# Merging the delta rule's inverted triangles for both directions at once, over four 32x32 array tiles in turn

## The chip, the cores and the metric

The kernel runs on one core of a Trainium2 chip. The metric is the device time of one execution in microseconds (us), from the first instruction to the last. Before the change three timed runs took 2108.64, 2114.71 and 2114.74 us, so the median is 2114.71 us.

The core has these engines: TensorE (PE in the rows; PEld is its loading of weights), VectorE (DVE), ScalarE (ACT), GpSimd (POOL) and SyncE (SP), which here only starts DMAs. Each engine takes its instructions in the order in which they stand in its own stream. TensorE's clock has two levels, 1.2 and 2.4 GHz; the rows give the granted clock as a share of the higher one, so 0.50 is 1.2 GHz.

## The reference, cut to what matters

Two layers of a diffusion backbone: a mixer (softmax attention beside a bidirectional gated delta rule) and a mixture of experts. 256 context tokens and 512 latent tokens make six token tiles of 128; the delta rule has 8 heads of width 64 and works in chunks of 64 tokens, forward and backward. Each chunk, head and direction needs the inverse of a unit lower triangle of 64x64:

```python
def gated_delta_chunked(q, k, v, g, beta, s0):
    ...
    lower = jnp.where(strict, jnp.einsum("bhnid,bhnjd->bhnij", kb, kc) * decay, 0.0)
    eye = jnp.eye(CHUNK, dtype=f32)
    tmat = lax.linalg.triangular_solve(lower + eye, jnp.broadcast_to(eye, lower.shape),
                                       left_side=True, lower=True, unit_diagonal=True)
    u = jnp.einsum("bhnij,bhnje->bhnie", tmat, vc * bc)
    ...
    s_final, o = lax.scan(step, s0, xs)

def hybrid_mixer(h_lat, h_ctx, lp, rope, ctx_out):
    ...
    for d in range(2):
        ...
        o_l, _ = gated_delta_chunked(*(rev(t) for t in (...)), s_c)
```

## The kernel before, in words

**The inverse.** The 64x64 triangle is cut into two 32x32 triangles on the diagonal and one 32x32 block beside them. With the diagonal inverses X0 and X1 and the block U, the missing corner of the inverse is -X1 U X0 (its mirror image in the other direction). `intra_batch` and `delta_intra` make the triangles (with the block kept in a tile `uo`), `delta_subst` inverts all 32x32 triangles of a batch on VectorE by substitution (31 steps of a product `sT` and a subtraction `sY`), and `delta_merge` makes the corner and writes the whole inverse to DRAM (`xad`). The token tiles go through in three batches of two tiles, `PAIRS`; below m0, m1 and m2 are the merges of the three batches, and s0 to s2 their substitutions. A layer has three batches and two directions, so six calls of `delta_merge`.

**One merge before.** The substitution's result goes to DRAM (`dy`, L825) and comes back in another layout as `yl` (L833, two DMAs per direction); VectorE transposes it in 32x32 blocks to `yt` (L834); ScalarE puts the diagonal blocks into the output tile `xm` (L838, two instructions). Then TensorE makes the first product in PSUM (L846, tile `mg`): 16 blocks (two token tiles by eight heads) on one 32x32 tile of the array, then ScalarE copies those 32 partitions, negated, to SBUF (L847), then the same 16 blocks for the other half of the partitions on another array tile and a second copy. The second product (L850) and its copies into `xm` (L851) follow in the same manner. One matmul of fp32 counts as two in the trace's rows, so 16 blocks are x32 there. Last the DMA to `xad` (L853).

**Buffers.** `yl`, `yt`, `xm` and the SBUF tile `mg` have one buffer each (`YL = 1`, `XM = 1`), so a merge waits for the one ahead of it. PSUM has three pools: three banks "a", three banks "c", and one buffer "s" of two banks. The two directions of a batch take a half of "s" each, except for m2 of layer 0, which takes banks of "c" (`MPS`). Attention's scores (`sc`, L603) also take "s", the only buffer of it.

**The order of work.** A string `ORDER` says in which order the pieces are written out (convolutions c, intra i, substitution s, projections n, merges m); a scheduler with a timeline model then sets the order on each engine, so instructions of several pieces interleave. After the merges come 12 delta steps (`delta_step`: pz L916, su L931, ks and pq L897, po L947), woven with attention slots and with the matmuls of the modulation (`aps` L264, from weights `araw`). The steps load the inverse (`lx` L864) and keys and values (`lk` L863) by the SP queue, behind the stores of the merges.

Of the kernel before, what the change touches and what calls it, by code (L numbers as in the profile page):

```python
# [23 lines left out]
P = 128  # L24
# [76 lines left out]
WH = 3  # L101
GV = 2
QS = 1
UO = 10
VR = 1
SB = 2
YB = 2
# [10 lines left out]
EV = (0,)  # L118
EP = (1, 3, 5, 7)
ST = 2  # L120
XM = 1
DDB = 2
FINP = (8, 9, 10, 11)
MPS = ((0, 1), (0, 1, 2))
ORDER = ("c4 c5 c6 c7 S i0 s0 i1 s1 i2 s2 c0 c1 c2 c3 Q n256 n0 x n512 m0 m1 c8 c10 c11 c9 n2304 m2",
         "c4 c5 c6 c7 S c0 i0 s0 i1 s1 c9 i2 s2 c1 c2 c3 Q n256 n0 x n512 m0 m1 c8 c10 n2304 c11 m2")
WP = 3
# [16 lines left out]
class Model:  # L144
# [638 lines left out]
    def delta_intra(self, tt, d, kk, sc, uo, xad, db, pool):  # L783

        nc = self.nc
        gx = pool.tile([P, NH, HD], F32, tag="gx", bufs=1, name="gx")
        nc.gpsimd.tensor_tensor(gx, sc["gr"][:, d, tt, :, None].to_broadcast([P, NH, HD]), self.C["run%d" % d][:, None, :].to_broadcast([P, NH, HD]), op=OP.mult)
        pg = self.psC("gb")
        nc.tensor.matmul(pg, self.C["same"], gx.rearrange("p h i -> p (h i)"), start=True, stop=True)
        dd = pool.tile([P, 512], F32, tag="dd", bufs=DDB, name="dd")  # L790
        d3 = dd.rearrange("p (h i) -> p h i", i=HD)
        nc.vector.tensor_tensor(d3, pg.rearrange("p (h i) -> p h i", i=HD), sc["gcum"][:, d, tt, :, None].to_broadcast([P, NH, HD]), op=OP.subtract)
        nc.vector.tensor_tensor(d3, d3, self.C["mask%d" % d][:, None, :].to_broadcast([P, NH, HD]), op=OP.min)
        nc.scalar.activation(dd, dd, AF.Exp)
        nc.gpsimd.tensor_tensor(d3, d3, sc["bp"][:, d, tt, :, None].to_broadcast([P, NH, HD]), op=OP.mult)
        u = pool.tile([P, 512], F32, tag="u", bufs=2, name="u")
        nc.vector.tensor_tensor(u, kk, dd, op=OP.mult)
        self.q("idd").dma_start(xad[tt, d, :, 1], dd)
        u3 = u.rearrange("p (h i) -> p h i", i=HD)
        qb = 1 - d  # L800
        nc.scalar.activation(uo, u3[:, :, 32 * qb:32 * qb + 32], AF.Copy)
        ud = pool.tile([P, NH, 32], F32, tag="ud", bufs=2, name="ud")
        nc.scalar.activation(ud, u3[:, :, 0:32], AF.Copy, scale=self.C["quad"][:, 0:1])
        nc.vector.scalar_tensor_tensor(ud, u3[:, :, 32:64], self.C["quad"][:, 1:2], ud, op0=OP.mult, op1=OP.add)
        src = ud
        if d == 1:
# [17 lines left out]
            nc.vector.tensor_tensor(Y[:, j + 1:32, 0:w], Y[:, j + 1:32, 0:w], T3, op=OP.subtract)  # L824
        self.q("iy").dma_start(dy.rearrange("h q r c -> (h q) r c"), Y)  # L825

    def delta_merge(self, tts, d, dy, us, xad, ps, pool):

        nc = self.nc
        yt = pool.tile([P, 2, NH, 32], F32, tag="yt", bufs=1, name="yt")  # L830
        yl = pool.tile([P, 2, NH, 32], F32, tag="yl", bufs=YL, name="yl")
        for t in range(2):
            self.q("ild").dma_start(yl[:, t], dy[:, 4 * t:4 * t + 4].rearrange("h q r c -> (q r) h c"))  # L833
        nc.vector.transpose(yt, yl)  # L834
        xb, xt = (yt, yl) if d == 0 else (yl, yt)
        x = pool.tile([P, 2, NH, HD], F32, tag="xm", bufs=XM, name="xm")
        for q in range(2):
            nc.scalar.activation(x[:, :, :, 32 * q:32 * q + 32], xb, AF.Copy, scale=self.C["quad"][:, q:q + 1])  # L838
        qa, qb = (0, 1) if d == 0 else (1, 0)
        cb = slice(32 * qb, 32 * qb + 32)  # L840
        g = pool.tile([P, 512], F32, tag="mg", bufs=1, name="mg")
        place = [(32 * (2 * c2 + qa), 32 * (2 * c2 + qb)) for c2 in range(2)]
        blocks = [(t, h, slice((t * NH + h) * 32, (t * NH + h + 1) * 32)) for t in range(2) for h in range(NH)]
        for ra, rb in place:
            for t, h, c in blocks:
                nc.tensor.matmul(ps[rb:rb + 32, c], us[tts[t], d][ra:ra + 32, h, :], xt[ra:ra + 32, t, h, :], start=True, stop=True, tile_position=(ra, rb))  # L846
            nc.scalar.activation(g[rb:rb + 32], ps[rb:rb + 32], AF.Copy, scale=-1.0)  # L847
        for ra, rb in place:
            for t, h, c in blocks:
                nc.tensor.matmul(ps[ra:ra + 32, c], g[rb:rb + 32, c], xb[rb:rb + 32, t, h, :], start=True, stop=True, tile_position=(rb, ra))  # L850
            nc.scalar.activation(x[ra:ra + 32, :, :, cb], ps[ra:ra + 32].rearrange("p (t h i) -> p t h i", t=2, h=NH), AF.Copy)  # L851
        a, b = tts
        self.q("ix").dma_start(xad[a:b + 1:b - a, d, :, 0].rearrange("t p f -> p t f"), x.rearrange("p t h i -> p t (h i)"))  # L853

    def step_load(self, s, vk, xad, qkd, need, pool):

# [134 lines left out]

    def intra_batch(self, b, us, dT, sc, xad, db, pool):
        kk = [self.delta_kk(tt, 1, dT, pool) for tt in PAIRS[b]]
        for d in range(2):
            for j, tt in enumerate(PAIRS[b]):
                us[tt, d] = pool.tile([P, NH, 32], F32, tag="uo", bufs=UO, name="uo")
                n = 4 * (2 * d + j)
                self.delta_intra(tt, d, kk[j], sc, us[tt, d], xad, db[:, n:n + 4], pool)

    def merge_batch(self, i, b, us, xad, dy, pool):  # L1000
        ps = self.psS("mg") if b in MPS[i] else None
        for d in range(2):
            self.delta_merge(PAIRS[b], d, dy[:, 8 * d:8 * d + 8], us, xad, ps[:, 512 * d:512 * d + 512] if ps is not None else self.psC("mg"), pool)


    def gate(self, mp, ps, n, dst):
# [495 lines left out]
    def layer(self, i, xsrc, rows, done, xstack, mod):  # L1502
# [20 lines left out]
        with self.pool("hp", B) as hp:  # L1523
            with self.pool("pj", B) as wp:
# [47 lines left out]
                with self.pool("pp", B) as pool, self.pool("q1", A) as p1:  # L1572
# [7 lines left out]
                    for op in ORDER[i].split():  # L1580
# [3 lines left out]
                        elif kind == "Q":  # L1584
                            query_norms()
                        elif kind == "c":
                            f = int(arg)
                            if f in (0, 4):
                                ss = self.psS("ss")
                            value_conv(f, pool) if f >= 8 else key_conv(f, ss, pool)  # L1590
                        elif kind == "i":
                            self.intra_batch(int(arg), us, dT, sc, xad, db[int(arg)], p1)
                        elif kind == "s":
                            self.delta_subst(int(arg), db[int(arg)], dy[int(arg)], p1)
                        elif kind == "m":
                            self.merge_batch(i, int(arg), us, xad, dy[int(arg)], p1)
# [172 lines left out]
```

## Time and profile before

| | |
|---|---|
| median of three runs | 2114.71 us |
| profiled execution | 2130.51 us |
| its span | 2128.7 us |
| mean granted clock of TensorE | 0.897 |
| TensorE busy | 1824.3 us (86%) |
| VectorE busy | 1272.6 us (60%) |
| ScalarE busy | 893.5 us (42%) |
| GpSimd busy | 839.5 us (39%) |

Busy shares are averages over stages with different limits. The stage of this change lies, in layer 0, between about 120 and 400 us of the span, and in layer 1 between about 1190 and 1466 us. In a row of the timeline, the first number is the start in us, the second the time in us; a bracket gives the idle time of the engine ahead of it and what ended that.

### The profile page before, as it was taken

Reading aid. Unit: us, or ns where it says so; the run is one execution under the profiler, and the core shown is the slowest. Engines: PE = TensorE matmul, PEld = TensorE weight load, DVE = VectorE, ACT = ScalarE, POOL = GpSimd, SP = SyncE. Lnnn points to the kernel's source line nnn. Section 1 sums busy time; section 2 is a strip of 40 time slices with the busy share of each in tenths; the row PEclk is TensorE's granted clock in tenths of the full one; section 3 lists DMA queues with packets and bytes.
Section 4 is the critical chain, followed back from the end, with each engine's and each line's share of the span. In section 5 each row is a group of like instructions: output and inputs, shape, how many; then the busy total and the mean of one; then the engine's idle time right before and its main releaser. Section 6 shows DMA issues by size and latency. Waiting matters only on the chain. (4 is left out here: it accounts for less than half of the span.)

```text
span 2128.7 us, 34974 instructions
## 1 busy us (share of the span) xinstructions
PE 1824.3 (86%) x13579; PEld 1349.2 (63%) x13579; DVE 1272.6 (60%) x2344; ACT 893.5 (42%) x1531; POOL 839.5 (39%) x915
## 2 busy tenths in 40 slices
PE   6998798888868789999978987767888769999995
PEld 4887687666657655565547876656566555566553
DVE  3469996566672645555546689963676443444443
ACT  3444245655541134444425543334464223444442
POOL 4456653244354323223326376520333632223221
PEclk9999897798988889999998988766998779999997
DMA  8222435787655588889924224356862568888872
GB/s 278 72 71 79 127 117 175 233 230 237 199 135 131 198 329 329 323 320 328 331 65 140 80 71 120 107 170 182 252 186 70 174 265 307 326 315 302 314 263 85
DMA packets 227684, 427.77 MB, mean 201 GB/s; under 512 B 83720, under 2 KB 157180, under 8 KB 202939
## 3 DMA queue, kind: packets, MB, share of 16 engines
q1 hardware_dynamic: 171547, 329.09, 45.9%
q0 software_dynamic: 33536, 72.59, 12.1%
q10 hardware_dynamic: 22432, 23.81, 3.3%
q8 instruction: 109, 1.79, 0.3%
q14 instruction: 60, 0.49, 0.1%
HBM read 386.82 MB, written 84.67 MB: 221 GB/s over the span
## 5 line engine op out<-in xcount | busy, mean ns | idle before, releaser
L1351 PE MATMUL pab<-w,xt 128*128 128x512 f32 x1024 | 465.5, 598 | 0.5 <-ACT xt L1345 0.5
L1351 PEld LDWEIGHTS pab<-w,xt 128*128 128x128 f32 x1024 | 189.7, 192 | 191.3 <-issue 186.5
L1405 POOL DMA_INDIRECT yd<-ey,idx x64 | 116.8, 1824 | 472.3 <-DMA yd<-ey,idx 196.9
L1372 DVE TENSOR_TENSOR gl<-gt,gh 128x256 fp32r<-128x256 f32 x64 | 27.1, 424 | 276.1 <-ACT gh L1371 272.5
L1330 DVE TENSOR_TENSOR w2l<-w,w2h 128x2048 fp32r<-128x2048 f32 x64 | 147.4, 2303 | 44.4 <-ACT w2h L1329 43.0
L1371 ACT ACTIVATE gh<-gt 128x256 fp32r<-128x256 f32 x64 | 24.5, 383 | 348.9 <-PE gt L1367 348.9
L238 PE MATMUL pn<-whi,hh 128*128 128x256 f32 (+1 forms) x432 | 133.9, 313 | 15.3 <-ACT gev L1541 11.4
L488 POOL TENSOR_TENSOR wlo<-wraw,whi 128x1024 fp32r<-128x1024 f32 (+1 forms) x44 | 112.0, 2547 | 82.8 <-ACT whi L487 81.9
L238 PE MATMUL po<-woh,m 128*128 128x512 f32 x320 | 113.0, 431 | 27.8 <-ACT woh L1068 20.6
L238 PE MATMUL pn<-whi,hl 128*128 128x256 f32 (+1 forms) x432 | 133.4, 313 | 0.7 <-DVE hl L349 0.4
L238 PE MATMUL pn<-wlo,hh 128*128 128x256 f32 (+1 forms) x432 | 133.0, 309 | 0.6 <-POOL wlo L488 0.6
L238 PE MATMUL pt<-hh,wlo 128*128 128x512 f32 (+1 forms) x352 | 125.4, 356 | 0.0
L238 PE MATMUL pt<-hh,whi 128*128 128x512 f32 (+1 forms) x352 | 124.3, 353 | 0.0
L238 PE MATMUL pt<-hl,whi 128*128 128x512 f32 (+1 forms) x352 | 123.8, 352 | 0.0
L1329 ACT ACTIVATE w2h<-w 128x2048 fp32r<-128x2048 f32 x64 | 121.7, 1902 | 0.0
L1393 PE MATMUL py<-w2h,gh 128*128 128x512 f32 x256 | 107.7, 421 | 4.4 <-DVE ey L1400 4.4
L1345 ACT ACTIVATE xt<-xt 128x512 f32<-128x512 f32 x128 | 69.7, 595 | 86.8 <-PE xt L1344 86.0
L517 DVE SCALAR_TENSOR_TENSOR dT<-xin,cw,dT 128x772 f32<-128x772 f32 x64 | 79.4, 1243 | 42.2 <-ACT dT L515 40.5
L238 PEld LDWEIGHTS pn<-whi,hh 128*128 128x128 f32 x432 | 90.1, 210 | 20.8 <-ACT gev L1541 12.1
L1393 PE MATMUL py<-w2l,gh 128*128 128x512 f32 x256 | 101.6, 397 | 0.0
L1393 PE MATMUL py<-w2h,gl 128*128 128x512 f32 x256 | 101.2, 395 | 0.0
L1344 PEld LDWEIGHTS xt<-cst,xe 128*128 128x128 f32 x512 | 67.9, 192 | 50.2 <-issue 29.8
(391 smaller groups left out, 4561.8 us busy)
## 6 DMA issues: line engine op xcount, KB each, us to landing
w<-w SPq DMA_DIRECT2D x192, 1024.0 KB, 10.0
araw<-ada_w POOLq DMA_DIRECT2D x40, 1024.0 KB, 9.3
wraw<-w_in SPq DMA_DIRECT2D x40, 512.0 KB, 4.1
lk<-vk SPq DMA_DIRECT2D x48, 256.0 KB, 7.2
lx<-xad SPq DMA_DIRECT2D x40, 256.0 KB, 9.3
araw<-ada_w SPq DMA_DIRECT2D x8, 1024.0 KB, 11.8
wr<-w_out SPq DMA_DIRECT2D x8, 1024.0 KB, 15.4
vk<-vr ACTq DMA_DIRECT2D x16, 384.0 KB, 3.2
```

The source lines that it names most:

```text
L238: self.nc.tensor.matmul(ps, a(k), b(k), start=(first and n == 0), stop=(last and n == 3 * nk - 1))
L488: getattr(nc, eng).tensor_tensor(lo, raw, hi, op=OP.subtract)
L517: nc.vector.scalar_tensor_tensor(dst, xin[:, tap:tap + 772], cw[:, tap, f:f + 1], dst, op0=OP.mult, op1=OP.add)
L1329: self.pin(nc.scalar.activation(hi, src, AF.Copy))
L1330: self.pin(eng.tensor_tensor(lo, src, hi, op=OP.subtract))
L1344: pin(nc.tensor.transpose(ps[:, k * P:(k + 1) * P], xe.rearrange("p (q k) -> p k q", k=8)[:, 4 * q + k, :], self.ident))
L1345: pin(nc.scalar.activation(xt[:, 4 * q:4 * q + 4, :], ps.rearrange("p (k n) -> p k n", k=4), AF.Copy))
L1351: self.pin(self.nc.tensor.matmul(pa.rearrange("p (a f) -> p a f", a=2), xt[:, k, :], w13[:, :, k, :], start=(k == 0), stop=(k == 7)))
L1371: pin(nc.scalar.activation(gh, p3, AF.Copy))
L1372: pin(nc.vector.tensor_tensor(gl, p3, gh, op=OP.subtract))
L1393: pin(self.nc.tensor.matmul(py[:, n * 512:(n + 1) * 512], a[:, j, :], b[:, c], start=(j + m == 0), stop=(j == 1 and m == 2)))
L1405: self.pin(self.nc.gpsimd.indirect_dma_start(out=yd, out_offset=bass.IndirectOffsetOnAxis(ap=idx, axis=0), in_=y, in_offset=None, bounds_c ...
```

## The change

`delta_merge` now takes both directions of a batch in one call. All four loads of `yl` are issued together into a tile of twice the size, one VectorE instruction transposes both, and one loop over the 16 blocks issues four matmuls per block: two directions by two halves, on the array tiles (row, column) (0, 32), (64, 96), (32, 0) and (96, 64). All four write to one PSUM bank, `pa`, on different partitions. One ScalarE instruction copies all 128 partitions. The second product goes in the same manner to the other bank of "s", `pb`, and is no longer copied by ScalarE: VectorE adds it, masked, to `xm`, one instruction per direction over all partitions, each followed by the store to `xad`.

The block U of both directions now shares one tile per token tile: direction d fills the partitions that start at 32d and 64 + 32d, by two ScalarE instructions of 32 partitions in place of one of 128. `UO` is 6 instead of 10. `XM` and `MPS` go: both output tiles `xm` have the one buffer that the tag has, and every merge takes "s".

```diff
-        qb = 1 - d
-        nc.scalar.activation(uo, u3[:, :, 32 * qb:32 * qb + 32], AF.Copy)
+        for r in (32 * d, 64 + 32 * d):
+            nc.scalar.activation(uo[r:r + 32], u3[r:r + 32, :, 32 - 32 * d:64 - 32 * d], AF.Copy)
...
-    def delta_merge(self, tts, d, dy, us, xad, ps, pool):
+    def delta_merge(self, tts, dy, us, xad, pool):
...
+        yt = pool.tile([P, 2, 2, NH, 32], F32, tag="yt", bufs=1, name="yt")
+        yl = pool.tile([P, 2, 2, NH, 32], F32, tag="yl", bufs=YL, name="yl")
+        for d in range(2):
+            for t in range(2):
+                n = 4 * (2 * d + t)
+                self.q("ild").dma_start(yl[:, d, t], dy[:, n:n + 4].rearrange("h q r c -> (q r) h c"))
         nc.vector.transpose(yt, yl)
...
+        xb, xt = (yt[:, 0], yl[:, 1]), (yl[:, 0], yt[:, 1])
+        x = [pool.tile([P, 2, NH, HD], F32, tag="xm", bufs=1, name="xm") for d in range(2)]
...
+        ps = self.psS("mg")
+        pa, pb = ps[:, :512], ps[:, 512:]
+        place = [(d, 32 * (2 * c2 + d), 32 * (2 * c2 + 1 - d)) for d in range(2) for c2 in range(2)]
...
-        for ra, rb in place:
-            for t, h, c in blocks:
-                nc.tensor.matmul(ps[rb:rb + 32, c], us[tts[t], d][ra:ra + 32, h, :], xt[ra:ra + 32, t, h, :], start=True, stop=True, tile_position=(ra, rb))
-            nc.scalar.activation(g[rb:rb + 32], ps[rb:rb + 32], AF.Copy, scale=-1.0)
...
+        for t, h, c in blocks:
+            for d, ra, rb in place:
+                nc.tensor.matmul(pa[rb:rb + 32, c], us[tts[t]][ra:ra + 32, h, :], xt[d][ra:ra + 32, t, h, :], start=True, stop=True, tile_position=(ra, rb))
+        nc.scalar.activation(g, pa, AF.Copy, scale=-1.0)
+        for t, h, c in blocks:
+            for d, ra, rb in place:
+                nc.tensor.matmul(pb[ra:ra + 32, c], g[rb:rb + 32, c], xb[d][rb:rb + 32, t, h, :], start=True, stop=True, tile_position=(rb, ra))
         a, b = tts
+        for d in range(2):
+            y = x[d][:, :, :, 32 - 32 * d:64 - 32 * d]
+            nc.vector.scalar_tensor_tensor(y, pb.rearrange("p (t h i) -> p t h i", t=2, h=NH), self.C["quad"][:, d:d + 1], y, op0=OP.mult, op1=OP.add)
+            self.q("ix").dma_start(xad[a:b + 1:b - a, d, :, 0].rearrange("t p f -> p t f"), x[d].rearrange("p t h i -> p t (h i)"))
```

The scheduler sets a new order from the substitutions on. On TensorE, at the end of m2 in layer 1, this stands before (each row is a run of matmuls; `mg<-yl,uo` and `mg<-yt,uo` are first products of the forward and the backward direction, `mg<-yt,mg` and `mg<-yl,mg` second products):

```order
L846 MATMUL mg<-yl,uo 32x32 x32
L850 MATMUL mg<-yt,mg 32x32 x32
L846 MATMUL mg<-yt,uo 32x32 x32
L850 MATMUL mg<-yl,mg 32x32 x32
L603 MATMUL sc<-ka,qs 128x512
```

and at the same place now (the first product's last rows and the second's first; a row is a direction's two halves):

```order
L848 MATMUL mg<-yl,uo 32x32 x2
L848 MATMUL mg<-yt,uo 32x32 x2
L848 MATMUL mg<-yl,uo 32x32 x2
L848 MATMUL mg<-yt,uo 32x32 x2
L852 MATMUL mg<-yt,mg 32x32 x2
L852 MATMUL mg<-yl,mg 32x32 x2
```

The number of matmuls is the same, 128 a batch; directions and halves now alternate, and two products take the place of four. On the SP queue, which stores and loads around m1 and m2 of layer 1, this stands before:

```order
L825 DMA dy_1_10416<-sY 128x1024
L833 DMA yl<-dy_1_10416 128x8x32 x2
L853 DMA xad_10410<-xm 128x2x512
L833 DMA yl<-dy_1_10416 128x8x32 x2
L853 DMA xad_10410<-xm 128x2x512
L825 DMA dy_1_10417<-sY 128x1024
L1018 DMA gw<-gd_10419 128x512 x2
L833 DMA yl<-dy_1_10417 128x8x32 x2
```

and now:

```order
L823 DMA dy_1_10394<-sY 128x1024
L834 DMA yl<-dy_1_10394 128x8x32
L857 DMA xad_10388<-xm 128x2x512
L834 DMA yl<-dy_1_10394 128x8x32 x3
L1018 DMA gw<-gd_10397 128x512 x2
L857 DMA xad_10388<-xm 128x2x512
L823 DMA dy_1_10395<-sY 128x1024
L834 DMA yl<-dy_1_10395 128x8x32
L857 DMA xad_10388<-xm 128x2x512
L834 DMA yl<-dy_1_10395 128x8x32 x3
```

Three of a batch's four loads stand behind the second direction's store of the batch ahead. In layer 0 the order on TensorE moves attention: before, 12 pairs of scores stand ahead of the first matmul of the delta steps, woven into m2; now all of m2 stands ahead of the first score, and 3 pairs ahead of the first delta step.

## Rows read from the trace of the kernel before

**Rows 1.** Windows: us, busy (instructions) of PE, PEld, DVE, ACT, POOL, clock, DMA, GB/s

```profile
120.00:345.00 225.00, 197.45 (x1860) 173.89 (x1859) 199.05 (x379) 89.99 (x171) 128.68 (x158) 0.92 0.36 101
345.00:400.00 55.00, 45.97 (x483) 37.49 (x483) 21.57 (x60) 36.59 (x89) 10.79 (x14) 0.53 0.63 185
1190.00:1405.00 215.00, 177.43 (x1448) 152.11 (x1446) 189.01 (x346) 84.26 (x156) 129.10 (x163) 0.86 0.35 101
1405.00:1466.00 61.00, 36.47 (x546) 32.30 (x547) 17.67 (x42) 21.64 (x37) 5.53 (x4) 0.53 0.48 139
...
395.00:600.00 205.00, 170.90 (x2571) 128.80 (x2569) 141.46 (x306) 115.39 (x226) 86.58 (x93) 0.91 0.78 225
```

**Rows 2.** Timeline of TensorE in layer 1, m1 to the first delta step

```profile
1411.72 1.03 PE L846 MATMUL mg<-yl,uo 32*32 32x32 f32 x16 [9.97 <-DMA yl<-dy]
...
1442.41 1.98 PE L846 MATMUL mg<-yl,uo 32*32 32x32 f32 x32 [2.94 <-DMA yl<-dy]
...
1462.42 1.91 PE L850 MATMUL mg<-yl,mg 32*32 32x32 f32 x32 [0.74 <-ACT xm L851]
1465.01 0.79 PE L603 MATMUL sc<-ka,qs 128*128 128x512 f32 x1 [0.68 <-ACT xm L851]
```

**Rows 3.** Timeline of TensorE at the full clock: one, two and four array tiles

```profile
282.43 1.19 PE L846 MATMUL mg<-yl,uo 32*32 32x32 f32 x32
...
412.34 0.92 PE L947 MATMUL po<-z,lx 64*64 64x64 f32 x26
...
1486.10 0.69 PE L931 MATMUL su<-w,lk 64*64 64x64 f32 x32
```

**Rows 4.** Timeline of ScalarE in layer 1, m2

```profile
1444.49 0.59 ACT L847 ACTIVATE mg<-mg 32x512 f32<-32x512 f32 x1 [4.38 <-PE mg L846]
1445.10 1.33 ACT L838 ACTIVATE xm<-yt,cst 128x512 f32<-128x512 f32 x2
```

**Rows 5.** Groups by line and form, whole span, VectorE and ScalarE

```profile
L920 DVE TENSOR_TENSOR w<-pz,scs 128x512 f32<-128x512 f32 x22 | 15.0, 681 | 4.5 <-PE pz L916 4.4
L801 ACT ACTIVATE uo<-u 128x256 f32<-128x256 f32 x24 | 9.9, 414 | 49.7 <-DVE u L797 49.3 <-PE mg L846 0.3
```

**Rows 6.** Tile xm: last line of the answer, the stores to xad

```profile
DMA to landing us min/median/max: 2.7/3.3/4.9
```

**Rows 7.** Timeline of SP, POOL and DVE in layer 1 around m1

```profile
1401.82 0.98 SPq L833 DMA_DIRECT2D yl<-dy  x2
...
1431.28 0.33 SPq L825 DMA_DIRECT2D dy<-sY  x1
...
1402.33 1.48 POOL L230 DMA_DIRECT2D araw<-ada_w  x2
...
1414.51 0.71 DVE L834 STREAM_TRANSPOSE yt<-yl 128x512 f32<-128x512 f32 x1 [9.11 <-DMA yl<-dy]
```

**Rows 8.** Timeline of SP, POOL and TensorE in layer 0 around m2

```profile
340.47 0.33 SPq L825 DMA_DIRECT2D dy<-sY  x1
...
388.98 0.50 SPq L863 DMA_DIRECT2D lk<-vk  x1
...
345.90 1.46 POOL L230 DMA_DIRECT2D araw<-ada_w  x2
...
351.93 1.54 PE L571 MATMUL kt<-cst,xl 128*128 128x128 f32 x6 [2.48 <-DMA xl<-qd]
353.26 0.64 PE L588 MATMUL qt<-cst,ql 128*128 128x128 f32 x2
...
357.00 0.55 PE L603 MATMUL sc<-ka,qs 128*128 128x256 f32 x1 [1.26 <-DVE qs L593]
...
391.88 0.58 PE L603 MATMUL sc<-ka,qs 128*128 128x256 f32 x1 [0.29 <-ACT pp L612]
...
393.79 0.58 PE L603 MATMUL sc<-ka,qs 128*128 128x256 f32 x1 [0.48 <-ACT pp L612]
...
395.16 0.47 PE L916 MATMUL pz<-lk,lx 64*64 64x64 f32 x2
```

More of the change, by code (lines that the diff above doesn't have):

```diff
@@ L103 @@
 QS = 1
-UO = 10
+UO = 6
 VR = 1
@@ L120 @@
 ST = 2
-XM = 1
 DDB = 2
 FINP = (8, 9, 10, 11)
-MPS = ((0, 1), (0, 1, 2))
 ORDER = ("c4 c5 c6 c7 S i0 s0 i1 s1 i2 s2 c0 c1 c2 c3 Q n256 n0 x n512 m0 m1 c8 c10 c11 c9 n2304 m2",
@@ L825, in delta_subst @@
         self.q("iy").dma_start(dy.rearrange("h q r c -> (h q) r c"), Y)
-    def delta_merge(self, tts, d, dy, us, xad, ps, pool):
+    def delta_merge(self, tts, dy, us, xad, pool):
         nc = self.nc
[L830 to L833, printed above, removed]
-        nc.vector.transpose(yt, yl)
[L835 to L840, printed above, removed]
+        yt = pool.tile([P, 2, 2, NH, 32], F32, tag="yt", bufs=1, name="yt")
[4 more added lines that the diff above has]
+                self.q("ild").dma_start(yl[:, d, t], dy[:, n:n + 4].rearrange("h q r c -> (q r) h c"))
+        nc.vector.transpose(yt, yl)
+        xb, xt = (yt[:, 0], yl[:, 1]), (yl[:, 0], yt[:, 1])
+        x = [pool.tile([P, 2, NH, HD], F32, tag="xm", bufs=1, name="xm") for d in range(2)]
+        for d in range(2):
+            for q in range(2):
+                nc.scalar.activation(x[d][:, :, :, 32 * q:32 * q + 32], xb[d], AF.Copy, scale=self.C["quad"][:, q:q + 1])
@@ L841, in delta_merge @@
         g = pool.tile([P, 512], F32, tag="mg", bufs=1, name="mg")
-        place = [(32 * (2 * c2 + qa), 32 * (2 * c2 + qb)) for c2 in range(2)]
+        ps = self.psS("mg")
+        pa, pb = ps[:, :512], ps[:, 512:]
+        place = [(d, 32 * (2 * c2 + d), 32 * (2 * c2 + 1 - d)) for d in range(2) for c2 in range(2)]
         blocks = [(t, h, slice((t * NH + h) * 32, (t * NH + h + 1) * 32)) for t in range(2) for h in range(NH)]
-        for ra, rb in place:
-            for t, h, c in blocks:
-                nc.tensor.matmul(ps[rb:rb + 32, c], us[tts[t], d][ra:ra + 32, h, :], xt[ra:ra + 32, t, h, :], start=True, stop=True, tile_position=(ra, rb))
-            nc.scalar.activation(g[rb:rb + 32], ps[rb:rb + 32], AF.Copy, scale=-1.0)
@@ L848, in delta_merge @@
[L848 to L851, printed above, removed]
+        for t, h, c in blocks:
+            for d, ra, rb in place:
+                nc.tensor.matmul(pa[rb:rb + 32, c], us[tts[t]][ra:ra + 32, h, :], xt[d][ra:ra + 32, t, h, :], start=True, stop=True, tile_position=(ra, rb))
@@ L852, in delta_merge @@
+        nc.scalar.activation(g, pa, AF.Copy, scale=-1.0)
+        for t, h, c in blocks:
+            for d, ra, rb in place:
+                nc.tensor.matmul(pb[ra:ra + 32, c], g[rb:rb + 32, c], xb[d][rb:rb + 32, t, h, :], start=True, stop=True, tile_position=(rb, ra))
         a, b = tts
-        self.q("ix").dma_start(xad[a:b + 1:b - a, d, :, 0].rearrange("t p f -> p t f"), x.rearrange("p t h i -> p t (h i)"))
+        for d in range(2):
+            y = x[d][:, :, :, 32 - 32 * d:64 - 32 * d]
+            nc.vector.scalar_tensor_tensor(y, pb.rearrange("p (t h i) -> p t h i", t=2, h=NH), self.C["quad"][:, d:d + 1], y, op0=OP.mult, op1=OP.add)
+            self.q("ix").dma_start(xad[a:b + 1:b - a, d, :, 0].rearrange("t p f -> p t f"), x[d].rearrange("p t h i -> p t (h i)"))
@@ L993, in intra_batch @@
         kk = [self.delta_kk(tt, 1, dT, pool) for tt in PAIRS[b]]
+        for tt in PAIRS[b]:
+            us[tt] = pool.tile([P, NH, 32], F32, tag="uo", bufs=UO, name="uo")
         for d in range(2):
             for j, tt in enumerate(PAIRS[b]):
-                us[tt, d] = pool.tile([P, NH, 32], F32, tag="uo", bufs=UO, name="uo")
                 n = 4 * (2 * d + j)
[L998 to L1003, printed above, removed]
+                self.delta_intra(tt, d, kk[j], sc, us[tt], xad, db[:, n:n + 4], pool)
     def gate(self, mp, ps, n, dst):
@@ L1595, in layer @@
                         elif kind == "m":
-                            self.merge_batch(i, int(arg), us, xad, dy[int(arg)], p1)
+                            self.delta_merge(PAIRS[int(arg)], dy[int(arg)], us, xad, p1)
                         elif kind == "x":
```

## The prediction

> **What bounds the kernel now.** I read the windows of the two stages first. Until 345 us in layer 0 and until 1405 us in layer 1 VectorE is busy 199.05 of 225 and 189.01 of 215 us [rows 1], 88% in both, and TensorE much the same; ScalarE is at 90 and 84 us and has room. Behind that, 345 to 400 and 1405 to 1466 us, no engine is full, above all in layer 1: TensorE 36.47 of 61 us, VectorE 17.67, ScalarE 21.64, and the granted clock is 0.53, near the lower level [rows 1]. Such a stage is bound by a chain of waits.
>
> The timeline of TensorE shows the chain [rows 2]. In layer 1 m1 begins at 1411.72, m2 at 1442.41, and the first score of attention comes at 1465.01, released by the last copy of m2, since it takes the same PSUM buffer. From 1429 us on nothing but merges stands in it: half a product (x32) of 1.9 us, a copy of 0.59 us [rows 4] and waits of some 0.7 us, eight times per batch. What shortens a merge there shortens the layer.
>
> **Part 1: the matmuls.** A run of 16 blocks on one array tile takes 1.19 us at the full clock [rows 3] and 1.91 us at the lower one [rows 2]. Does a matmul on another tile run beside it? No merge of before shows it, but the delta steps do [rows 3]. The su matmuls alternate over four 64x64 tiles: x32 in 0.69 us; less the last one's own 0.22 us that is 0.47 over 31 steps, 15 ns a step, 61 ns on each tile. The po matmuls alternate over two tiles: (0.92 - 0.22) over 25 steps, 28 ns a step, 56 ns on each tile. So a tile keeps its own pace whatever the others do. For 32x32 blocks the pace is (1.19 - 0.19) / 31 = 32 ns, so four in turn need a step of 8 ns, and su's pairs of load and matmul were issued at 15 ns or faster. I take 1.95 us for a whole product at the lower clock and 1.25 at the full one; the bounds are four runs of before, 4 x 1.91 less 3 x 0.24 of ends, 6.9 us (at the full clock 4.2), and one run, 1.91.
>
> The Trainium skill speaks against this. Its page "TensorEngine Tiling (Array Packing)", section Restrictions and Gotchas, says that different row tiles cannot access the same PSUM bank simultaneously; here four row tiles write one bank, pa or pb. By that rule a product would cost the serial bound, 6.9 us, and it is the first rival below. The trace so far disagrees for two row tiles: po writes one bank from two of them and keeps 56 ns a tile, where su, with a bank per row tile, keeps 61 [rows 3].
>
> **Part 2: the chain of one merge at the lower clock, now.** Operands there to the first product's end 2.0; copy 0.59 + 0.15 of waits; second product 2.0; VectorE's addition for the forward direction 0.7, taking the row of a VectorE instruction of 128x512 from PSUM, 681 ns [rows 5]; start of the store 0.1 and its landing 3.3 [rows 6]. The landing counts, because both directions have one xm buffer: ScalarE fills it for the backward direction only when the forward one is stored. Then 1.33 for that [rows 4], 0.7 for the second addition, and 0.3 of waits. Sum 11.2 us, against 1465.01 - 1442.41 = 22.6 for m2 before [rows 2]: 11.4 less, of which a new wait of 5 us on the store is already paid.
>
> **Part 3: layer 1 in whole.** m1's loads were issued at 1401.82, 0.5 us ahead of 2 MB of araw [rows 7], and landed about 9.9 us later, when TensorE [rows 2] and VectorE (at 1414.51, 9.11 us idle [rows 7]) went on; a quiet transfer lands in 3.3 [rows 6]. Three of the four loads now stand behind the second store of m0, so I leave them at 1412: the same collision. Both transposes, 2 x 0.71 [rows 7], to 1413.4; first product to 1415.4, other matmuls 3.2, second product to 1420.6. VectorE needs 1431.28 - 1415.2 = 16 us from m1's transpose to the end of s2 [rows 7]; one conv step of 1.0 and a second transpose of 0.7 are out of that now, so 14.3 us, to 1427.7. The first addition of m1 stands two instructions ahead of that end in VectorE's new order, so its store leaves at 1428.4, not 1421: landed 1431.7, second addition 1433.8, loads of m2 issued to 1435.4, landed 1438.7, transposed 1440.1, and 11.2 us to the first score: 1451. That is **14 us** earlier than 1465. If m1's loads escape the araw transfer it is 6 more, 20.
>
> **Part 4: layer 0.** s2 ends with dy at 340.47 [rows 8]. VectorE is full up to there, and gets four additions of 0.7 and a transpose of m1 that came later, 3.5 us: 344. Landing 3.3, four loads of 0.5, and a landing next to araw (started at 345.90 [rows 8]) between 3.3 and 9.9 us, I take 6.6: 356; transposes 1.4, product 2.0, kt and qt 2.2 [rows 8], then copy hidden, second product and the tail of part 2, 8.4: the last store leaves at 370 instead of just ahead of 388.98 [rows 8]. The delta steps begin 18.5 us earlier.
> But attention, which began at 357.00 and ran inside m2, must wait until 370 for buffer s. 12 pairs of scores stood ahead of the first delta step, 3 stand there now, so 8 to 9 small units are owed. One alone takes 393.79 - 391.88 = 1.91 us [rows 8]: 16 us. TensorE is idle for 34 of 205 us in the steps that follow [rows 1], so a part will fit into gaps; I take half, 8. Net **10.5 us**, between 2 and 18.5.
>
> **Part 5: what is hidden.** The copies of U: 24 instructions of 414 ns become 48; if half the partitions take as long, 9.9 us more on ScalarE [rows 5], in stages where it is busy under 42% and VectorE stands ahead of it. If that cover fails it is at most 5 us a layer. m0 in both layers and m1 in layer 0 stand among convolutions and projections; TensorE saves about 6 us a batch there, but VectorE sets the pace, so nothing is taken, and its four to six additions are in the sums.
>
> **Sum.** 14 + 10.5 = 24.5 us. The profiled execution took 2130.5 us, its span 2128.7; it would be 2106. It lies 15.8 us above the median of the timed runs, and most rows here are waits that do not scale, so I take the difference from the median: 2114.7 - 24.5 = **2090 us**.
>
> **The rivals.**
> *One bank serialises the four row tiles* (7 in 100). A product stays at 6.9 us, 5 more for each. In layer 1 m1 has 7 us of slack behind VectorE and loses 3, m2 loses 10: 14 becomes 1. In layer 0 m2 loses 10 of 10.5. Time 2113, no change. For it: no row shows four row tiles in one bank. Against it: po.
> *Layer 0 gives nothing* (25 in 100): the owed attention goes at 1.91 us each since one score buffer sets its pace, 16 of the 18.5 us. Gain 14 + 2: 2099. For it: in rows 8 the scores of 391.88 and 393.79 follow on ScalarE's exponentials. Against it: TensorE's idle time.
> *Both layers give all* (20 in 100): m1's loads escape araw, and delta steps set the pace in layer 0: 20 + 18.5, so 2076.
> *The single xm buffer makes it slower* (6 in 100): stores of the forward direction fall into the araw transfers and land in 9.9 us, and VectorE, in order, stands behind the second addition. Layer 1: 6.6 for each of m1 and m2 and 6.6 for the loads behind them, 14 - 20 = -6; layer 0: 18.5 - 6.6 - 16 = -4. Time 2125. It decides from landings of about 8 us per store on. Against it: araw waits for its two buffers once these are full, and the store line has 4.9 at most [rows 6].
> The rest, 42 in 100, is the forecast, with its own range 2080 to 2100.
>
> **Numbers.** What a measurement of this kernel can tell from no change is about 0.3%, 2108.4 to 2121.1. Faster: nearly all of the forecast, of layer 0 nothing and of both layers, 0.83. Same: the serial bank, half of the slow rival and the edges, 0.12. Slower 0.05. The range reaches from below the full gain to just short of no gain: 2068 to 2112.
>
> **What would show it.** In the profile after: a product of all blocks as one run of x128 (fp32 counts twice) in about 1.9 us at clock 0.50 and 1.25 at 1.00; 4 or 7 us says the bank serialises. In layer 1 the first score at about 1451, and ahead of m2's second addition a ScalarE wait on the store of xm. In layer 0 the first score near 370 and the first delta step near 377, with small units of attention spread over the first four steps. I am wrong if the loads of yl for m1 or m2 land later than 10 us after issue, if the delta steps in layer 0 end where they did, or if VectorE idles behind the additions long enough to move dy.

## The result and the profile after

The change made the kernel slower. Eight runs took 2125.89 us in the median (2123.24 to 2132.89), the kernel before 2115.93 us over its runs of the same comparison; the ratio is 1.0054, with a 95% interval of 1.0034 to 1.0074. By the ratio that is 11 us more, where 25 less was forecast. The profiled execution took 2123.24 us with a span of 2121.4 us. Executions of the kernel before spread from 2108 to 2130 us, so a difference between two single profiles is read below only where it is larger than some 8 us or stands in several kernels. The first profile of before is of an execution of 2130.51 us; e5 is a second one, of 2119.95 us, nearer the median, and stands beside the profile after where times count.

The merges themselves do what was forecast. The windows of after that answer to [rows 1] (us, busy and instructions of PE, PEld, DVE, ACT, POOL, granted clock, DMA share, GB/s):

```profile
345.00:400.00 55.00, 23.29 (x511) 17.12 (x511) 19.10 (x48) 23.00 (x57) 16.37 (x19) 0.66 0.82 224
395.00:600.00 205.00, 163.75 (x2335) 120.74 (x2326) 136.16 (x298) 110.92 (x225) 80.97 (x90) 0.91 0.72 212
1405.00:1466.00 61.00, 19.12 (x690) 15.14 (x689) 35.92 (x85) 16.70 (x28) 10.85 (x12) 0.61 0.61 180
```

TensorE's busy time around m2 has halved in both layers, but only a part of that in layer 0 is the merges. Their own matmuls (windows of tile `mg`) take 9.27 us of the third window instead of 30.06, and 3.52 us of the first instead of 20.52; the rest of the first window's fall is attention that now comes later. In layer 1 the timeline of TensorE in m2 reads, to answer [rows 2]:

```profile
1459.45 0.26 PE L848 MATMUL mg<-yt,uo 32*32 32x32 f32 x2 [4.90 <-DVE yt L835]
...
1461.07 0.30 PE L848 MATMUL mg<-yt,uo 32*32 32x32 f32 x4
...
1469.91 0.76 PE L601 MATMUL sc<-ka,qs 128*128 128x512 f32 x1 [5.39 <-DVE xm L856]
```

A first product over all 16 blocks, four tiles and both directions (all but its first four matmuls as the rows count them, which had run at 1454.23) takes 1.9 us to the end of its last row, 1461.37; the granted clock is 0.50 in it:

```profile
1459.40:1461.40 2.00, 1.92 (x124) 1.78 (x124) 0.00 (x0) 1.33 (x2) 0.00 (x0) 0.50 0.03 8
```

ScalarE then shows the new wait on the store of `xm`, 6.25 us idle ahead of the backward fill:

```profile
1461.41 0.60 ACT L849 ACTIVATE mg<-mg 128x512 f32<-128x512 f32 x1 [0.60 <-PE mg L848]
1468.26 1.33 ACT L840 ACTIVATE xm<-yl,cst 128x512 f32<-128x512 f32 x2 [6.25 <-DMA xad<-xm]
```

Layer 0 is where it went wrong. The waits of TensorE there, 340 to 615 us (engine, line and tile that waited, for what: us in all, times, longest):

```profile
PE sc L601 <- ACT pp L610: 12.5, 12, 2.8
PE mg L848 <- DVE yt L835: 12.3, 1, 12.3
PE aps L262 <- DMA araw<-ada_w: 11.1, 7, 5.7
PE sc L601 <- DVE xm L856: 9.2, 1, 9.2
...
PE mg L848 <- DMA yl<-dy: 7.3, 1, 7.3
```

The two waits of `mg` and the one of `sc` on `xm` are 29 us in which TensorE stands with attention's matmuls queued behind m2, first because its stream is in order, then because m2 holds buffer s. So from 340 to 380 us it is busy 10 us of 40 in the changed kernel,

```profile
340.00:380.00 40.00, 10.00 (x298) 8.93 (x298) 12.40 (x30) 10.36 (x22) 10.34 (x13) 0.63 0.65 182
```

and 34 in the kernel before (e5):

```profile
340.00:380.00 40.00, 33.63 (x408) 29.49 (x407) 16.88 (x47) 24.37 (x55) 10.69 (x13) 0.59 0.66 203
```

Attention has 48 score units in layer 0, done in a fixed order: 16 small ones (two key tiles, 128x256) and then 32 large ones (six, 128x768). VectorE's maximum `mx` marks each. In the changed kernel, the first unit, the fourth, the sixteenth and the last (the transpose ahead of them waited 17 us; the profile names `cr`, a load issued behind m2's four on the same queue, and in e16 the same wait, 17.17 us, ends on `yl` itself; one transpose now waits for all four loads, and in e10, which has the same merges, these landed 6.3 to 15.1 us after their issue):

```profile
362.34 1.25 DVE L835 STREAM_TRANSPOSE yt<-yl 128x1024 f32<-128x1024 f32 x1 [17.21 <-DMA cr<-conv_w]
...
378.68 0.42 DVE L605 TENSOR_REDUCE mx<-sc 128x1 f32<-128x256 f32 x1 [0.95 <-PE sc L601]
...
386.80 0.42 DVE L605 TENSOR_REDUCE mx<-sc 128x1 f32<-128x256 f32 x1 [2.49 <-PE sc L601]
...
437.55 0.41 DVE L605 TENSOR_REDUCE mx<-sc 128x1 f32<-128x256 f32 x1
...
613.68 0.95 DVE L605 TENSOR_REDUCE mx<-sc 128x1 f32<-128x768 f32 x1
```

In the kernel before (e5), the first, the sixteenth and the last:

```profile
359.43 0.42 DVE L607 TENSOR_REDUCE mx<-sc 128x1 f32<-128x256 f32 x1
...
407.79 0.41 DVE L607 TENSOR_REDUCE mx<-sc 128x1 f32<-128x256 f32 x1
...
592.78 0.96 DVE L607 TENSOR_REDUCE mx<-sc 128x1 f32<-128x768 f32 x1
```

The first delta step begins at 383.73 us after,

```profile
383.73 0.44 PE L920 MATMUL pz<-lk,lx 64*64 64x64 f32 x2 [0.64 <-DMA lx<-xad]
```

and at 395.69 before (e5):

```profile
395.69 0.47 PE L916 MATMUL pz<-lk,lx 64*64 64x64 f32 x2
```

So the steps start 12 us earlier, the small units are done 30 us later, and the stage ends 21 us later.

Counted from s2's store of `dy`, the stage takes 270.7 us after and 251.1 in e5. Cut at the first step and at the sixteenth unit, it gives these windows of TensorE (us, busy and instructions, granted clock, DMA share, GB/s), after:

```profile
342.94:383.73 40.79, 9.67 (x281) 0.59 0.73 201
383.73:437.55 53.82, 38.61 (x596) 0.77 0.99 285
437.55:613.68 176.13, 147.44 (x2044) 0.93 0.61 178
```

and before (e5):

```profile
341.67:395.69 54.02, 45.98 (x507) 0.55 0.62 186
395.69:407.79 12.10, 11.29 (x189) 0.90 1.05 263
407.79:592.78 184.99, 153.22 (x2309) 0.94 0.78 228
```

TensorE has 15 us less work, and is idle 34 us more: 23 of them ahead of the first step (31.1 against 8.0), 14 between that and the sixteenth unit (15.2 against 0.8, at a granted clock of 0.77 against 0.90), and 3 less behind it.

### The profile page after: what moved, and what is told of

Its sections match the earlier page's. It is cut to its first block, busy times and chain, and to the rows that moved or that the text cites. A ratio compares the mean times of both kernels' runs of the same rounds, so it can differ in the third digit from the quotient of the medians.

```text
span 2121.4 us, 34943 instructions
## 1 busy us (share of the span) xinstructions
PE 1758.6 (83%) x13579; PEld 1287.2 (61%) x13579; DVE 1272.5 (60%) x2350; ACT 882.0 (42%) x1513; POOL 839.4 (40%) x915
## 5 line engine op out<-in xcount | busy, mean ns | idle before, releaser
L610 ACT ACTIVATE pp<-sc,mx 128x768 f32<-128x768 f32 (+1 forms) x80 | 65.3, 816 | 83.5 <-DVE mx L605 83.2
```

What stands on the lines that cost most here:

```text
L610: self.pin(self.nc.scalar.activation(u.p[:, :u.nk * P], u.ps[:, :u.nk * P], AF.Exp, bias=u.mx, accum_out=u.sm))
```

## The experiments

Eighteen kernels were run, because the forecast was wrong and its cause open; e5 is the kernel before once more. Ratios are to the kernel before in the same comparison; 0.1% is 2.1 us.

**e1: the buffer alone.** The kernel before, but m2 of layer 0 takes buffer s.

```diff
-MPS = ((0, 1), (0, 1, 2))
+MPS = ((0, 1, 2), (0, 1, 2))
```

> The kernel before with one edit: m2 of layer 0 takes the halves of buffer s, as all other merges do, instead of two banks of c (MPS). Theory A, late attention: the change loses in layer 0, because m2 holds the only score buffer, so the score units of attention that ran inside m2 are put off into the delta steps. Then this kernel, with the merges of before, starts attention some 30 us later (near 390 us instead of 357), carries 3 pairs of scores ahead of the first delta step instead of 12, and is slower than before by 15 to 30 us (2131 to 2146). Rival B, the single xm buffer and its store wait, or rival C, VectorE's additions: neither is in this kernel, so it is within 5 us of before.

2145.83 us, ratio 1.012 (1.0091 to 1.015): 25 us lost without any of the new merges. The sixteenth and the last unit in layer 0:

```profile
446.35 0.42 DVE L607 TENSOR_REDUCE mx<-sc 128x1 f32<-128x256 f32 x1
...
617.92 0.95 DVE L607 TENSOR_REDUCE mx<-sc 128x1 f32<-128x768 f32 x1
```

Its first delta step, at 390.85 us, is 5 us ahead of that of e5, and its stage ends 25 us later. Theory A passes; B and C, which are not in this kernel, are not needed for a loss of this size.

**e2: m2 of layer 0 in banks of c.**

```diff
-        ps = self.psS("mg")
-        pa, pb = ps[:, :512], ps[:, 512:]
+        ps = None if apart else self.psS("mg")
+        pa, pb = (self.psC("mg"), self.psC("mg")) if apart else (ps[:, :512], ps[:, 512:])
```

> The changed kernel with one edit: m2 of layer 0 takes two banks of c for its two products, so the scores need not wait for it. In the new order five pairs of scores stand ahead of the first delta step (three in the changed kernel), still behind m2's matmuls on TensorE. Theory A: attention starts at about 366 instead of 378 us, and 2 to 3 units less are owed: 6 to 12 us less than the changed kernel, 2114 to 2120. Rivals B and C: within 4 us of the changed kernel (2126).

2125.47 us, 1.0041 (1.0019 to 1.0063): no gain worth the name, a miss for theory A and the number that B and C gave. The first unit came at 369.4, but the pairs still stood behind m2's matmuls on TensorE, and these waited 20 us for operands. Freeing the buffer without the order isn't enough.

**e3: m2 of layer 0 in the old form.**

```diff
+                            if i == 0 and arg == "2":
+                                for d in range(2):
+                                    self.delta_merge_one(PAIRS[2], d, dy[2][:, 8 * d:8 * d + 8], us, xad, self.psC("mg"), p1)
```

> The changed kernel, but m2 of layer 0 alone is done in the form of before (one direction after the other, one array tile at a time, copies by ScalarE, banks of c); the other five merges stay in the new form. Scores are woven into m2 again, six pairs ahead of the first delta step. Theory A: layer 0 loses nothing against before (the delta steps begin near 390 us and end where they did), and layer 1 keeps its gain of 13 us or more: 2100 to 2110. Rivals B and C: the waits and additions that cost are in the five other merges too, so at least half of the loss stays: 2118 or more.

2130.71 us, 1.0056 (1.0036 to 1.0075): a miss for theory A as it stood, in the range of B and C. The first unit is early, at 363.7, but the steps start at 380.3 with 6 pairs ahead; the sixteenth unit came at 439.4 and the last at 613.0, as in the changed kernel. An early first score alone buys nothing.

**e4: a second output tile.**

```diff
+             pool.tile([P, 32, 32], F32, tag="sB", bufs=SB, name="xn")...
```

> The changed kernel, but the output tile of the backward direction takes one of the two buffers of the tile sB (same size) instead of the one buffer of xm, so that it is filled without a wait on the forward direction's store. Rival B: 5 us less in each of m1 and m2 of layer 1 and in m2 of layer 0, 10 to 15 us less than the changed kernel (2111 to 2116). Theory A: layer 1 gets its 5 to 8 us at most; layer 0 starts its delta steps some 5 us earlier with the same units of attention owed, so nothing comes of it there: 2117 to 2122.

2135.94 us, 1.0078 (1.0052 to 1.0104): both theories missed. In layer 1 the wait is gone: from the last `dy` store to the first unit's maximum 18.2 us instead of 23.7. Still the kernel is no faster than the changed one; by the ratios it is 5 us slower, which is within their intervals. Its first step in layer 0 is the earliest of all, 376.6, with 4 pairs ahead.

**e5: before again.**

> The kernel before once more, unchanged, for a second profile: the first profiled execution of it took 2130.5 us, 13 above its median. In the traces so far the stage of layer 1 from the end of s2 to the last po of the delta steps is 213.9 us before and 190.8 in the changed kernel, yet 203.6 in e1, whose layer 1 is that of before. If the first profile was the odd one, the stage is 203 to 206 here, the layer-1 gain of the change 12 to 15 us, and the last score of layer 0 still comes about 253 us behind the end of s2.

2119.95 us in one run. Layer 1, from s2's store of `dy` to the last po, took 204.5 us, as expected, where the first profile had 213.9. In layer 0 the last unit's maximum came 251.1 us behind s2's store.

**e6 and e7: one layer each.** Each has the functions of the kernel before for one layer (`OLD` is 0 in e6, 1 in e7).

```diff
+                            if i == OLD:
+                                self.merge_batch(i, int(arg), us, xad, dy[int(arg)], p1)
+                            else:
```

> The change in layer 1 alone: layer 0 has the triangles, merges and buffers of before (MPS, ten uo tiles), and its order on TensorE has 12 pairs of scores ahead of the first delta step again. Theory A (layer 0 alone loses, layer 1 gains as forecast): 12 to 15 us less than before, 2102 to 2106. Rival D, the gain of layer 1 is given back in its delta steps or behind: within 4 us of before.

2109.53 us, 0.9955 (0.9934 to 0.9977): 10 us less than before, between the forecasts of A and D and nearer to A.

> The change in layer 0 alone: layer 1 as before. Theory A: all of the loss and none of the gain, 20 to 25 us above before, 2138 to 2142. Rival D: 8 to 12 us above before, like the changed kernel.

2141.74 us, 1.0113 (1.0081 to 1.0145), as theory A said. So the change gains 10 us in layer 1 and loses 24 in layer 0; the sum, 14, agrees with the 11 of both within their intervals. Rivals B and C don't explain a loss in layer 0 alone: their waits and additions stand in layer 1 too, and layer 1 gains. In layer 1 of e6 SP stores `dy` of s2, and TensorE runs the first score, at

```profile
1423.21 0.32 SPq L825 DMA_DIRECT2D dy<-sY  x1
```

```profile
1444.73 0.77 PE L603 MATMUL sc<-ka,qs 128*128 128x512 f32 x1 [5.43 <-DVE xm L858]
```

21.5 us apart; in e5 33.4 (1431.14 to 1464.56).

**e8 to e11: order of m2, and the w_out loads.** e8 ties m2's first product on TensorE behind the third pair of scores:

```diff
+        if self.scores == 3:
+            for m in self.late:
+                self.tc.add_manual_dep(m.ins, mm.ins.name, ...)
```

> As e2 (m2 of layer 0 in two banks of c), and in addition the matmuls of its first product are ordered on TensorE behind the third pair of scores, so that kt, qt and the first scores no longer stand behind matmuls that wait for yl. Eight pairs of scores stand ahead of the first delta step. In all traces with the scores ahead or behind, the attention stream of layer 0 takes 232 to 238 us from the first score to the last. Theory A, made precise: the stream sets the end of the stage, and TensorE's order (m2's matmuls, waiting for operands, ahead of attention) is what starts it late. First score at about 357 us, last at about 592, delta steps no matter when, layer 1 as in the changed kernel: 2104 to 2110. Rival E: delta steps that start 15 us earlier put their loads and the 3 MB of w_out ahead of araw, TensorE waits for araw, and the stream stretches to 245 to 250 us as in e3: 2114 to 2122.

2125.84 us, 1.0043 (1.0023 to 1.0063), above both forecasts. e9 adds that the loads of w_out stand behind those of later steps:

```diff
+        self.tc.add_manual_dep(dma.ins, self.loaded.ins.name, ...)
```

> As e8, and the three w_out loads of each layer are ordered on the SP queue behind the loads of delta steps 5 to 7, instead of behind those of step 1. Rival E: the stream is no longer stretched; 8 to 15 us less than e8. Theory A alone: the same as e8 within 4 us.

2111.83 us, 0.9971 (0.9955 to 0.9987): 14 us less than e8, as rival E said; how much of that is E's stands below. e10 has the w_out order alone:

> The changed kernel with the w_out loads ordered behind those of delta steps 5 to 7, and nothing else. Rival E: the delta steps and araw of layer 0 get the queue 10 us earlier, and the loss of layer 0 shrinks by 8 to 15 us: 2111 to 2118. Theory A: the stream starts at 378 as before and takes 235: within 4 us of the changed kernel (2126).

2133.14 us, 1.0072 (1.0051 to 1.0092): nothing of E's gain, and by the ratios 4 us above the changed kernel. e11:

```diff
+        if bare:
+            ... (the two stores)
+            return
```

> The changed kernel without m2's two products and additions in layer 0 (the corner of the inverse of those two token tiles is left out; loads, transpose, fills and stores stay). Nothing of m2 is on TensorE or in buffer s. This bounds what any form of m2 could give. Theory A: first score at 357, last at 592, 20 us less than the changed kernel, 2103 to 2108. Rival E: delta steps from about 370 on, stream of 245 or more, 2113 to 2120.

2142.59 us, 1.0109 (1.0085 to 1.0133): all theories missed. Without m2's products TensorE and buffer s are free, and the kernel is slower still. Its trace shows a third way in which m2 holds attention up, by VectorE: the one transpose stands 17.62 us in VectorE's stream, waiting for the loads, and the `qs` that the first score needs comes behind it,

```profile
362.62 1.25 DVE L835 STREAM_TRANSPOSE yt<-yl 128x1024 f32<-128x1024 f32 x1 [17.62 <-DMA yl<-dy]
```

```profile
368.37 0.58 PE L601 MATMUL sc<-ka,qs 128*128 128x256 f32 x1 [14.10 <-DVE qs L591]
```

so that the first score comes at 368 and not at 357 (in e8, too, at 365.19, behind a transpose that waited 17.64 us). TensorE also waits 33.2 us for `araw`, against 11.1 in the changed kernel. The first step is at 383.05; the sixteenth and the last unit are at

```profile
448.06 0.43 DVE L605 TENSOR_REDUCE mx<-sc 128x1 f32<-128x256 f32 x1
...
620.31 0.95 DVE L605 TENSOR_REDUCE mx<-sc 128x1 f32<-128x768 f32 x1
```

A second thing is mixed into these four. The scheduler's order in layer 1 shifts with edits in layer 0. In e8 the last two `dy` stores are 44.8 us apart,

```profile
1399.38 0.45 SPq L828 DMA_DIRECT2D dy<-sY  x1
1444.18 0.34 SPq L828 DMA_DIRECT2D dy<-sY  x1
```

and in e9 36.2:

```profile
1393.33 0.33 SPq L828 DMA_DIRECT2D dy<-sY  x1
1429.50 0.41 SPq L828 DMA_DIRECT2D dy<-sY  x1
```

e8, e10, e11, e13 and e14 have 66 VectorE instructions between the ends of the two substitutions, and 44.1 to 44.8 us; after, e9 and e16 have 58, and 36.2 to 38.2. These 8 us explain more than half of e9's gain over e8 and all that e10 lost. What the later w_out loads give beside them is small or nothing.

**e12 to e16: hold the steps.** The first matmuls of delta step 0 are ordered behind the k-th pair of scores, nothing else:

```diff
+                if s == 0 and self.pairs < 12:
+                    self.held.append(mm)
...
+        if self.pairs == 12:
+            for m in self.held:
+                self.tc.add_manual_dep(m.ins, mm.ins.name, ...)
```

> The changed kernel with one edit: in layer 0 the first matmuls of delta step 0 (pz) are ordered on TensorE behind the twelfth pair of scores, as they stood before the change; 36 units of attention are left for the phase of the steps instead of 45. Theory N: the units are worked off in their order, so each one put off leaves a large unit (six token tiles) at the end of the stage; phases with 36, 40 and 45 units took 197.5, 213 and 229 us from the first pz to the last score, 3.5 us a unit. First pz at about 404 instead of 384, last score 404 + 197.5 = 601 instead of 614: although the steps start 20 us later, 12 us less than the changed kernel, 2112 to 2117. Rival F: the steps' start sets the end, and holding them costs what it delays: 2138 or more.

2112.10 us, 0.9968 (0.9945 to 0.999): with the steps started later it is 18 us faster than the changed kernel by the ratios, and faster than the kernel before. F falls. How much of the 18 us is layer 0's stays open. Its trace, of an execution 6.5 us above its median, shows no gain there: from s2's `dy` store to the last unit 270.9 us, as in the changed kernel (270.7), with 23.4 us of TensorE's waits for `araw` instead of 11.1. And its order in layer 1 has a small gain of its own (32.3 us between the `dy` stores), so e16 holds behind the tenth pair, where that order is the changed kernel's:

> The changed kernel with the first pz of layer 0 ordered behind the tenth pair of scores (e12: the twelfth). Its order in layer 1 is that of the changed kernel; in e12 one instruction of VectorE stood elsewhere there and the last substitution ended some 4 us sooner, so that e12 doesn't isolate layer 0, and this does. Theory N, with 38 units in the phase instead of 45 at 3.5 us each, and a start 12 us later: 10 to 14 us less than the changed kernel, 2111 to 2117. Rival F (the steps' start sets the end): 2136 to 2140. Rival G (what e12 gained came from layer 1 alone): 2122 to 2128.

2121.38 us, 1.0019 (0.9999 to 1.0039): 7 us less than the changed kernel, with an interval of about 6 each way. The sign is N's, F is out again, the size is between N and G. The first step stands 12 us later, at 395.90, and the last unit came 12 us earlier (4 of which are an earlier end of s2 in this execution):

```profile
415.94 0.41 DVE L610 TENSOR_REDUCE mx<-sc 128x1 f32<-128x256 f32 x1
...
601.58 0.95 DVE L610 TENSOR_REDUCE mx<-sc 128x1 f32<-128x768 f32 x1
```

e13 and e15 hold behind the sixteenth pair, e14 behind the twelfth.

> As e8 (m2 of layer 0 in banks of c, behind the third pair of scores), with the first pz of layer 0 ordered behind the sixteenth pair: all small units are done ahead of the steps, 32 are left. Theory N: first score 367, first pz about 404, phase 197.5 - 4 x 3.5 = 183.5, last score 588 against 603 in e8: 15 us less than e8, 2108 to 2114. Rival F: 16 us more than e8, 2140.

2131.21 us, 1.0069 (1.0042 to 1.0095); a miss, by some 20 us, 8 of them its layer 1.

> As e11 (m2's products and additions of layer 0 left out), with the first pz of layer 0 ordered behind the twelfth pair of scores. e11 had 6 pairs ahead, delta steps from 383 on, and TensorE waited 33 us for araw: slower than the changed kernel by 17 us. Theory N and rival E (early steps put their loads ahead of araw) both say that it gains: N alone 6 x 3.5 less a start 12 us later, 9 us less than e11, 2134; with E the waits for araw fall to the 11 us of before too and it gains 25 to 30, 2113 to 2118.

2126.01 us, 1.003 (1.0008 to 1.0052): 17 us less than e11, between the two forecasts.

> As e6 (the change in layer 1 alone), with the first pz of layer 0 ordered behind the sixteenth pair of scores instead of the twelfth; nothing else moves. Theory N: four units less in the phase, 14 us less, for a start 8 us later: 3 to 7 us less than e6, 2102 to 2107. Rival F: 8 us more than e6, 2118.

2118.56 us, 0.9999 (0.9982 to 1.0016): 9 us more than e6, as F said. The first step stands at 406.11 and the last unit at 602.02, 196 us behind it, though 4 units fewer were left than in e6, where it was 197:

```profile
406.11 1.66 PE L927 MATMUL pz<-lk,lx 64*64 64x64 f32 x26
```

```profile
602.02 0.95 DVE L612 TENSOR_REDUCE mx<-sc 128x1 f32<-128x768 f32 x1
```

So N has a floor: beyond twelve pairs, holding the steps costs what it delays. This rests on the one pair e15 and e6; e13 against e8 (5 us by the ratios) points the same way, within the intervals.

**e17 and e18: the w_out loads once more**, on e6 and on e12.

> As e6 (the change in layer 1 alone), with the w_out loads ordered behind the loads of delta steps 5 to 7. Less the 8 us by which VectorE's order in layer 1 differs between e8 and e9, the w_out loads were worth 6 us there, and 1 to 0 in e10: 2104 to 2109 by theory N with E as a small term; rival E as a large term: 2095 to 2101.

2118.62 us, 0.9996 (0.998 to 1.0012): 9 us worse than e6, a miss for both.

> As e12, with the w_out loads ordered behind the loads of delta steps 5 to 7: the candidate that keeps the new merges in both layers. Theory N with E as a small term: 2106 to 2112; rival E as a large term: 2098 to 2104.

2114.41 us, 0.9976 (0.9962 to 0.999): as e12, a little above the forecast of N. The collision with the w_out loads is not the cause; why e17 lost 9 us isn't settled.

**What the runs say together.** Two streams share TensorE in layer 0, the 12 delta steps and the attention units. Where the steps start last and all small units are done (e13, e15), the last unit comes 196 to 197.5 us after the first step. Where few pairs are ahead (e1, e11), it comes 172 us after the sixteenth unit. Taking the later of the two, first step + 196 or sixteenth unit + 172, as the end, the other kernels read:

| kernel | pairs ahead | first step | 16th unit | + 196 | + 172 | last unit |
|---|---|---|---|---|---|---|
| before (e5) | 12 | 395.7 | 407.8 | 592 | 580 | 592.8 |
| e6 | 12 | 394.1 | 406.2 | 590 | 578 | 591.2 |
| after | 3 | 383.7 | 437.5 | 580 | 610 | 613.7 |
| e3 | 6 | 380.3 | 439.4 | 576 | 611 | 613.0 |
| e9 | 8 | 390.9 | 426.5 | 587 | 599 | 601.3 |
| e16 | 10 | 395.9 | 415.9 | 592 | 588 | 601.6 |

By this reading the steps were the bound before, with attention 12 us behind it; after, attention is. It is a description, not a law; its two numbers are taken from e1, e11, e13 and e15. It holds within about 4 us for these but e16, which is 10 us later (both of its bounds lie close together), and for e10. e2, e8, e12, e14 and e18 come 12 to 14 us later than it says, e7 and e17 7 to 8, and e4 11 us earlier. What the mixed streams lose there stays open. One lead: between 340 and 615 us TensorE waits 17 to 23 us for `araw` in the five that come 12 to 14 us late, and 10 to 12 in e5, e6, after, e9 and e10; but e3, which fits, waits 27.

No kernel was clearly the best: e6 (0.9955), e12 (0.9968), e9 (0.9971) and e18 (0.9976) beat both kernels, and their intervals overlap.

## Why the prediction was wrong, step by step

*Part 1, the matmuls: right.* 1.9 us for a product at clock 0.50 (forecast 1.95). m2's second product in layer 0 ran from 367.36 to 368.64 us, 1.28 us (forecast 1.25), at a granted clock of 0.98:

```profile
367.20:368.40 1.20, 1.20 (x125) 1.05 (x126) 0.64 (x3) 1.16 (x3) 0.68 (x1) 0.98 1.04 348
```

Four row tiles wrote one bank side by side, so the serial bank, the first rival, is out, and with it the rule of the Trainium skill (TensorEngine Tiling (Array Packing), Restrictions and Gotchas) as a statement on time: by it a product would have shown 6.9 us.

*Part 2, the chain of a merge: right.* From its transposed operands (1459.45) to the first score m2 of layer 1 takes 10.5 us, forecast 11.2. The wait on the single `xm` is there; e4, which takes it away, gives 5.5 us back in m2 of layer 1 (forecast 5). The forward stores of `xm` in layer 1 land 2.8 to 2.9 us after their issue, as the waits of ScalarE end on them, not the 8 from which the fourth rival decides: it named nearly the time that came, 2125, for a reason that the trace refutes.

*Part 3, layer 1: right.* From s2's `dy` store to the first score 22.0 us in the changed kernel (1447.88 to 1469.91), against 23.3 forecast and 33.4 in e5. e6 measures 10 us of gain (5 to 14), forecast 14.

*Part 4, layer 0: the step that failed.* Three of its terms were off, and the second weighs most.
The steps were to start 18.5 us earlier. They start 12 earlier: m2's four loads, issued from 345.76 us on, were transposed from 362.34 on, where 356 was forecast. These 16.6 us are more than the 10 that the prediction named as a sign of being wrong: the term for the landing, 6.6 us, was too small, and all four loads must land before the one transpose.
The owed attention was 8 to 9 units at 1.91 us, 16 us in all, and "a part will fit into gaps; I take half, 8". Hardly any did: behind the sixteenth unit TensorE is idle 28.7 us, against 31.8 in e5. 1.91 us is a small unit with nothing else on TensorE, at a granted clock of 0.50. Among the delta steps the small units took 4.2 us each ((437.55 - 386.80) / 12), where matmuls of the steps and of the modulation stand between them and TensorE idles 15 us. The sixteenth unit came 30 us later than before, not 8. The 32 large units behind it then took 176.1 us instead of 185.0; that these 9 us are the steps' lead, given back, fits but is shown by no run alone.
And the lead of the steps was counted as a gain of the stage. Before, the steps were the later stream, but by the table only by some 12 us, so by that reading it could have given no more than that before attention set the end, even with no unit owed. The bounds of the net, 2 to 18.5, had no loss in them: the lower one assumed that at worst all 16 us stayed.
The measured term is a loss of 24 us (e7, 17 to 31) where a gain of 10.5 stood: 34.5 us, nearly all of the 36 between 2090 and 2126. That the loss lies in layer 0, and comes when attention is put off behind m2, is shown (e7, e6, e1); how its size divides among the waits, the order of the units and `araw` is not.

*Part 5: the copies of U and m0, m1 hidden.* Nothing contradicts it: s2's store in layer 0 starts at 342.9 us after and at 341.7 in e5. A copy of 32 partitions takes as long as one of 128 did (414 ns in the median against 417), so ScalarE does pay the 9.9 us. No run took the copies alone.

*The rivals.* "Layer 0 gives nothing" had the right place and the right direction, with a price per unit less than half of the measured one; slower than before by layer 0's attention was not among the cases, so 0.05 for slower was too little. "Both layers give all" is out by e7.

## What to carry to other kernels

When a producer is made faster ahead of two streams that share an in-order engine, find out first which stream ends last and by how much: the start of the other is worth at most that margin. Price work that is put off at what it costs where it will land, mixed with the other stream, not at what it costs alone, and take no cover from an engine's idle share unless a row shows the work running there. When several loads are put behind one instruction, ask what else stands behind that instruction in its engine's order. Measure a change by its places (here by layer) before believing its sum, and see whether the schedule far from the edit moved too.

## What was not expected of the hardware

Operands of 512 KB came late: 16.6 us from the first issue of m2's four loads in layer 0 (345.76) to the transpose, beside 2 MB of `araw` and the loads of attention, where a store of `xm`, of the same size, lands in 2.8 us at m2 of layer 1. And the spread of single executions, 2108 to 2130 us for one unchanged kernel, was nearly as wide as the largest difference read here, 25 us.
